# Transposed attention weights and two modulation parts of layer 0, in a two-layer DiT block on one Trainium2 core

## The chip, the cores and the metric

The kernel runs on one NeuronCore of a Trainium2 chip. The metric is device time in microseconds (us) of one execution, lower is better. The kernel before takes 2725.24 us, the median of three runs (2724.99 to 2725.42).

## The reference, cut to what matters

Everything is float32. Two layers work on `x` (1024 tokens by 1024 channels); the first also reads a context of 256 tokens. Each layer takes six modulation vectors (shift, scale, gate for the mixer; the same for the experts) from a conditioning vector:

```python
def adaln(cond, w, b):                       # w: 1024 x 6144 per layer
    m = jax.nn.silu(cond) @ w + b
    return jnp.split(m[..., None, :], 6, axis=-1)

sh1, sc1, gt1, sh2, sc2, gt2 = adaln(c, w_mod[layer], b_mod[layer])
hx = modulate(x, norm_mix_g[layer], sh1, sc1)     # rmsnorm(x)*(1+scale)+shift
...                                               # layer 0: mLSTM heads and window attention
p = jax.nn.softmax(jnp.concatenate([s_loc, s_ctx, s_sink], axis=-1), axis=-1)
out = einsum(p[..., :w3], vw) + einsum(p[..., w3:], vc)
...
x = x + gt1 * yx
x = x + gt2 * ec_moe(modulate(x, norm_ffn_g[layer], sh2, sc2), *moe)
```

Window attention has 8 heads of width 64, blocks of 128 queries, and for each block up to 3 x 128 local keys, 256 context keys and a sink that enters the sum of the softmax only. Layer 1's mixer is a chunked gMLP. Both layers end in a mixture of 16 experts.

## The kernel before, in words

To keep float32 accuracy at one pass per column, a large operand is split into a high part (type fp32r, written by ScalarE) and the rest (low part, by VectorE or GpSimd), and a product is three matmuls: high x high, low x high, high x low. Small products stay plain float32.

The program is written in a framework that traces it and then orders each engine's instructions itself: a planner with estimated costs takes, on each engine, the first ready instruction in the order of the text, and sets the semaphores. Each engine and each DMA queue (SP, ACT, POOL) then runs its list in order. So the text gives priorities, not the final order. A tile pool has a number of buffers per tag; a new tile waits until a buffer of that tag is released by its last reader.

**Start** (`start`, L182). Two context tiles and eight tiles of rows of `x`, each 128 x 1024, lie in the pool `xp`, tag `xt`, ten buffers (L185, L190). `start_mod` (L259) computes shift and scale of the first mixer: eight weight tiles of 1 MB on SP's queue, 32-column float32 matmuls (L272), and at k = 2 the transposes of the context (L166). Then `heads_context` (L219) projects the context for four heads: per head a key and a value projection (`proj`, L298, 24 matmuls of 256 columns each), a convolution on VectorE, and a store. Each projection's weight is 512 KB on SP's queue into a ring of two (`wraw`), split by ScalarE (L70) and VectorE (L71). Between projections, two of sixteen row steps are issued (`more`, L245, L254): four transposes (L213) of 128 columns of the rows, and the modulated copy, split (L174 to L179). A half of the rows (four `xt` tiles) is read until its eighth step.

**Attention** (`layer0_a` L551, `attention` L445). For each of 4 pairs of heads and 8 query blocks: scores of two heads into two-bank PSUM tiles (L462 to L466), row maximum (L472), exponential with sum (L475), reciprocal of the sum (L478). Then `dg`, the identity scaled by that column (L480), and a plain float32 product of each 128 x 128 tile of exponentials `P` with `dg` (L492), which transposes and scales at once, back into the score tile. The result is split (L494, L495) and multiplied by the values (L501, L502). There are 4 or 5 such tiles for a head and block, 304 in all.

Between these steps `fill` issues other work: 288 projection steps of three matmuls (query, head inputs, gates) in portions of 4, 2 and 3 a block, and with 9 of 28 of them one step of the modulation. `mod_part` (L660) computes one of the ten remaining vectors (layer 0 parts 2 to 5, layer 1 parts 0 to 5): eight steps, each a 512 KB weight tile `wm` on POOL's queue (ring of two, L667) and four 32-column float32 matmuls (L670), and a ninth step that adds the bias (L676) and either stores the vector (parts 2 and 5) or transposes it into columns (L683, L684).

```python
            mods = itertools.chain(*(self.mod_part(lm, pa, pt, i // 6, i % 6) for i in range(2, 12)))
            def fill(n):
                for _ in itertools.islice(work, n):
                    i = next(steps)
                    if 9 * (i + 1) // 28 > 9 * i // 28:
                        next(mods, None)
```

After attention come the mLSTM (`layer0_b`), the experts of layer 0, the gMLP and the experts of layer 1.

Of the kernel before, what the change touches and what calls it, by code (L numbers as in the profile page):

```python
# [8 lines left out]
F32 = mybir.dt.float32  # L9
# [4 lines left out]
ALU = mybir.AluOpType  # L14
# [7 lines left out]
KD = 8  # L22
# [16 lines left out]
class Kernel:  # L39
# [142 lines left out]
    def start(self, rings):  # L182
        nc, I = self.nc, self.I
        with ExitStack() as late:
# [29 lines left out]
                        self.modulated(ps, k, sm, gs[:, 0, :], mc[:, 0, 0:8], self.hH[:, k, sl], self.hL[:, k, sl])  # L214
                        yield

            self.heads_context(late, pt, Ws, rows())

    def heads_context(self, s, pt, Ws, more):  # L219

        nc = self.nc
        hc = (self.cH, self.cL)
# [12 lines left out]
        for hd in range(4):  # L235
            W = Ws.pop(0) if Ws else self.w_in(512 + hd * 128)
            acc = self.pa.tile([128, 512], F32, tag="acc", name="acc")
            self.proj(acc[:, :NCTX], W, hc, 0, NCTX)
            pad = cpool.tile([128, NCTX + 4], F32, tag="cpad", name="cpad")
            nc.vector.memset(pad[:, 0:2], 0.0)  # L240
            nc.vector.memset(pad[:, NCTX + 2:NCTX + 4], 0.0)
            nc.scalar.activation(pad[:, 2:2 + NCTX], acc[:, :NCTX], AF.Copy)
            kc = cpool.tile([128, NCTX], F32, tag="kcT", name="kcT")
            self.conv_silu(pad, NCTX, 4 + hd, kc)
            list(itertools.islice(more, 2))  # L245
            W = Ws.pop(0) if Ws else self.w_in(1024 + hd * 128)
            acc = self.pa.tile([128, 512], F32, tag="acc", name="acc")
            self.proj(acc[:, :NCTX], W, hc, 0, NCTX)
            vc = cpool.tile([128, NCTX], F32, tag="vcT", name="vcT")
            nc.scalar.activation(vc, acc[:, :NCTX], AF.Copy)  # L250
            if kept:
                store(*kept)
            kept = hd, kc, vc
            list(itertools.islice(more, 2))  # L254
        store(*kept)
        for _ in more:
            pass

    def start_mod(self, cs, cT, sm, pt):  # L259
# [185 lines left out]
    def attention(self, hp, c, Q, fill):  # L445
# [6 lines left out]
        for n in range(NT):  # L452
# [17 lines left out]
            for i in range(2):  # L470
# [16 lines left out]
            for i in range(2):  # L487
                if i:
                    fill(self.FILLS[1])
                P, dg = Ps[i]  # L490
                for j in range(nt):
                    nc.tensor.matmul(S[i][:, 512 - nl + j * 128:640 - nl + j * 128], P[:, j * 128:(j + 1) * 128], dg, start=True, stop=True)  # L492
# [58 lines left out]
    def layer0_a(self, rings):  # L551
        nc, I = self.nc, self.I
        with ExitStack() as s:
# [60 lines left out]
            mods = itertools.chain(*(self.mod_part(lm, pa, pt, i // 6, i % 6) for i in range(2, 12)))  # L614
# [4 lines left out]
            def fill(n):  # L619

                for _ in itertools.islice(work, n):
                    i = next(steps)
                    if 9 * (i + 1) // 28 > 9 * i // 28:
                        next(mods, None)

            for c in range(4):
# [30 lines left out]
                                        kh[base:base + 64, c0:c0 + n].bitcast(F32), op=ALU.subtract)  # L657


    def mod_part(self, pool, pa, pt, layer, w):  # L660


        nc, I = self.nc, self.I
        acc = pa.tile([128, 512], F32, tag="acc", name="acc")[:, 0:256]
        for k in range(KD):
            wm = pool.tile([128, D], F32, tag="wm", name="wm")
            nc.gpsimd.dma_start(out=wm, in_=I["w_mod"][layer, k * 128:(k + 1) * 128, D * w:D * (w + 1)])  # L667
            lhs = self.silw[:, k].rearrange("p a s -> p (a s)")
            for j in range(4):
                nc.tensor.matmul(acc[32 * j:32 * j + 32, :], lhs, wm[:, 256 * j:256 * (j + 1)], start=(k == 0), stop=(k == KD - 1))  # L670
            yield
        rows = pool.tile([128, 256], F32, tag="mrows", name="mrows", bufs=1)
        bias = pool.tile([128, 256], F32, tag="mbias", name="mbias", bufs=1)
        b = I["b_mod"]
        nc.gpsimd.dma_start(out=bias, in_=bass.AP(tensor=b.tensor, offset=b.offset + 6 * D * layer + D * w, ap=[[256, 4], [0, 32], [1, 256]]))
        nc.vector.tensor_tensor(rows, acc, bias, op=ALU.add)  # L676
        if w % 3 == 2:
            i = 2 * layer + w // 3
            nc.gpsimd.dma_start(out=self.s_gt[i].rearrange("(j c) -> j c", j=4), in_=rows[0:128:32, :])
        else:  # L680
            tr = pt.tile([128, 512], F32, tag="tr", name="tr")
            for t in range(2):
                nc.tensor.transpose(tr[:, t * 128:(t + 1) * 128], rows[:, t * 128:(t + 1) * 128], self.ident)  # L683
            nc.vector.tensor_copy(self.modc[:, layer, 8 * w:8 * w + 8].rearrange("p (j t) -> p j t", t=2),  # L684
                                  tr[:, 0:256].rearrange("p (t j r) -> p j t r", t=2, j=4)[:, :, :, 0])
        yield


# [1012 lines left out]
```

## Time and profile before

| | |
|---|---|
| median of 3 runs | 2725.24 us (2724.99 to 2725.42) |
| the profiled execution | 2720.4 us, span 2718.6 us, mean granted clock 0.968 |
| TensorE (PE) busy | 2529.9 us, 93% of the span |
| VectorE (DVE) / ScalarE (ACT) / GpSimd (POOL) busy | 1879.9 / 1511.4 / 626.0 us |
| chain that ended last, by engine | PE 80%, DVE 8%, DMA 4%, issue 4%, ACT 3% |
| start, to about 104 us; attention, about 165 to 590 us | inside the span |

PE is busy nearly everywhere, and records of matmuls overlap: what a matmul costs is the distance between starts, not its own duration. PEld is the load of weights, which overlaps. PEclk is TensorE's granted clock as a share of 2.4 GHz (0.5 is 1.2 GHz). "x8" is a merged group of records; a 128-column plain float32 product leaves two records, a transpose one.

### The profile page before, as it was taken

What the parts mean: (1) busy time and instruction counts of PE and PEld (TensorE: products, weight loads), DVE (VectorE), ACT (ScalarE), POOL (GpSimd) and SP (SyncE); (2) the same over time, 40 slices, a digit from 0 to 9 for tenths busy, and PEclk for the clock granted to TensorE, in tenths of its full rate; (3) what the DMA queues carried; (4) which work ended last, traced back from release to release, by engine and by line L of the source; (5) the groups of instructions that cost most, each with busy time, mean ns of one, the idle gap of its engine ahead of it and who ended that gap; (6) DMA issues with size and microseconds to landing.
All of it is one profiled execution on the core that took longest, in us unless ns stands there. A gap on an engine that the chain in (4) does not pass through costs nothing.

```text
span 2718.6 us, 35149 instructions
## 1 busy us (share of the span) xinstructions
PE 2529.9 (93%) x12847; PEld 2005.4 (74%) x12847; DVE 1879.9 (69%) x2830; ACT 1511.4 (56%) x2258; POOL 626.0 (23%) x413
## 2 busy tenths in 40 slices
PE   5999999998895999999998999999995999999996
PEld 3767777777774788888776887888884788888774
DVE  5566656567737999999885184116505899999887
ACT  4344344334424888888775223232322888888774
POOL 0010111115421222221102434533451021231001
PEclk8999999999996999999999999999997999999998
DMA  7344554457166999999966323342335999999995
GB/s 261 103 128 141 152 160 142 144 185 265 48 238 234 352 388 380 387 380 386 374 215 202 101 67 119 117 147 70 101 108 190 376 373 388 380 381 382 359 363 186
DMA packets 241642, 644.02 MB, mean 237 GB/s; under 512 B 18609, under 2 KB 85341, under 8 KB 240445
## 3 DMA queue, kind: packets, MB, share of 16 engines
q1 hardware_dynamic: 205136, 530.52, 52.3%
q0 software_dynamic: 25840, 89.99, 11.7%
q10 hardware_dynamic: 10492, 21.26, 2.3%
q8 instruction: 101, 1.65, 0.2%
q14 instruction: 73, 0.59, 0.1%
HBM read 589.06 MB, written 50.02 MB: 235 GB/s over the span
## 4 chain that ended last, share of the span: by engine, by line
PE 80%; DVE 8%; DMA 4%; issue 4%; ACT 3%; POOL 1%; POOLq 0%; ACTq 0%; SPq 0%; DVEq 0%
PE g L1134 13%; PE u L1134 13%; PE d L1134 12%; PE acc L298 8%; PE acc L1444 7%; PE acc L1518 6%; PE acc L1466 6%; PE S L492 2%; PE acc L805 2%; PE acc L670 2%; DMA wm<-in_w_mod_dram 1%; PE tr L1164 1%; DVE s2k L1460 1%; PE tr L1208 1%; PE O L501 1%
## 5 line engine op out<-in xcount | busy, mean ns | idle before, releaser
L71 DVE TENSOR_TENSOR ml<-mraw,mh 128x1024 fp32r<-128x1024 f32 x750 | 875.3, 1222 | 61.7 <-ACT mh L70 61.2
L70 ACT ACTIVATE mh<-mraw 128x1024 fp32r<-128x1024 f32 x750 | 769.3, 1064 | 138.6 <-PE g L1134 67.8
L71 POOL TENSOR_TENSOR wl<-wraw,wh 128x1024 fp32r<-128x1024 f32 (+1 forms) x132 | 253.6, 1930 | 349.8 <-ACT wh L70 349.8
L70 ACT ACTIVATE wh<-wraw 128x1024 fp32r<-128x1024 f32 (+1 forms) x163 | 143.0, 893 | 311.0 <-issue 123.6
L1232 POOL DMA_INDIRECT s_x<-xe,idx x28 | 66.9, 2388 | 655.0 <-ACT hidH L1210 394.4
L1134 PE MATMUL g<-mh,xH 128*128 128x512 f32 x512 | 206.4, 403 | 1.4 <-ACT xH L1169 1.4
L1134 PE MATMUL g<-ml,xH 128*128 128x512 f32 x512 | 205.3, 401 | 1.5 <-DVE ml L71 1.4
L1134 PE MATMUL g<-mh,xL 128*128 128x512 f32 x512 | 204.4, 399 | 0.0
L1134 PE MATMUL u<-ml,xH 128*128 128x512 f32 x512 | 203.4, 397 | 0.2
L1134 PE MATMUL u<-mh,xL 128*128 128x512 f32 x512 | 202.2, 395 | 0.0
L1134 PE MATMUL u<-mh,xH 128*128 128x512 f32 x512 | 202.2, 395 | 0.0
L1134 PE MATMUL d<-ml,hidH 128*128 128x512 f32 x496 | 197.5, 398 | 5.0 <-DVE ml L71 4.9
L1152 POOL DMA_INDIRECT xe<-s_xr,idx x32 | 137.7, 4303 | 270.7 <-ACT mh L70 131.0
L1134 PE MATMUL d<-mh,hidH 128*128 128x512 f32 x496 | 198.2, 400 | 1.6 <-DVE o L1229 1.6
L1134 PE MATMUL d<-mh,hidL 128*128 128x512 f32 x496 | 196.3, 396 | 0.0
L1444 PE MATMUL acc<-wh,h2k 128*128 128x512 f32 x512 | 163.7, 400 | 1.8 <-DVE h2k L1426 1.7
L1466 PE MATMUL acc<-h2k,wh 128*128 128x512 f32 x512 | 161.5, 396 | 0.0
L298 PE MATMUL acc<-hH,wh 128*128 128x512 f32 (+1 forms) x368 | 155.4, 422 | 1.6 <-DVE mrows L676 0.5
L1518 PE MATMUL acc<-wh,s2k 128*128 128x512 f32 x480 | 152.1, 397 | 0.0
L298 PE MATMUL acc<-hL,wh 128*128 128x512 f32 (+1 forms) x368 | 145.7, 396 | 0.0
L298 PE MATMUL acc<-hH,wl 128*128 128x512 f32 (+1 forms) x368 | 145.7, 396 | 0.0
L667 POOL DMA_DIRECT2D wm<-in_w_mod_dram x80 | 42.7, 534 | 406.6 <-PE acc L670 382.1
(469 smaller groups left out, 5238.9 us busy)
## 6 DMA issues: line engine op xcount, KB each, us to landing
mraw<-in_moe_w_down_dram SPq DMA_DIRECT2D x128, 1024.0 KB
mraw<-in_moe_w_gate_dram SPq DMA_DIRECT2D x126, 1024.0 KB
mraw<-in_moe_w_up_dram SPq DMA_DIRECT2D x124, 1024.0 KB
wm<-in_w_mod_dram POOLq DMA_DIRECT2D x80, 512.0 KB, 4.2
wraw<-in_gm_w_in_dram SPq DMA_DIRECT2D x64, 512.0 KB
wraw<-in_gm_w_out_dram SPq DMA_DIRECT2D x32, 512.0 KB
wraw<-in_ab_w_in_dram SPq DMA_DIRECT2D x30, 512.0 KB
wm<-in_w_mod_dram SPq DMA_DIRECT2D x8, 1024.0 KB
```

What stands on the lines that cost most here:

```text
L70: nc.scalar.activation(h, src, AF.Copy)
L71: i = (nc.gpsimd if eng == "pool" else nc.vector).tensor_tensor(l, src, h.bitcast(F32), op=ALU.subtract)
L298: nc.tensor.matmul(acc, a[:, k, :], b[:, k, c0:c0 + n], start=(k == 0 and i == 0), stop=(k == KD - 1 and i == 2))
L492: nc.tensor.matmul(S[i][:, 512 - nl + j * 128:640 - nl + j * 128], P[:, j * 128:(j + 1) * 128], dg, start=True, stop=True)
L670: nc.tensor.matmul(acc[32 * j:32 * j + 32, :], lhs, wm[:, 256 * j:256 * (j + 1)], start=(k == 0), stop=(k == KD - 1))
L805: nc.tensor.matmul(acc, a[:, k, t * 128:(t + 1) * 128], b[:, k % 2, :], start=(k == 0 and i == 0), stop=(k == 3 and i == 2))
L1134: nc.tensor.matmul(acc[:, sl], a[:, k, :], b[:, sl], start=(k == 0 and i == 0), stop=(k == KD - 1 and i == 2))
L1152: f = nc.gpsimd.indirect_dma_start(out=xe, out_offset=None, in_=self.s_xr[layer], in_offset=bass.IndirectOffsetOnAxis(ap=self.idx[e], axis=0))
L1232: nc.gpsimd.indirect_dma_start(out=self.s_x[layer], out_offset=bass.IndirectOffsetOnAxis(ap=self.idx[e], axis=0), in_=o, in_offset=None, c ...
L1444: nc.tensor.matmul(acc[t], a[k][:, ts], b[:, k2, :], start=(k == 0 and i == 0), stop=(k == KD - 1 and i == 2))
L1466: nc.tensor.matmul(acc, a[:, k, :], b[k], start=(k == 0 and i == 0), stop=(k == KD - 1 and i == 2))
L1518: nc.tensor.matmul(acc, a[:, ts], b[k2], start=(c == 0 and i == 0), stop=(c == 15 and i == 2))
```

## The change

Three edits. The tiles `P` are scaled by VectorE, in place, and then transposed plainly. Parts 2 and 3 of layer 0 (gate of the mixer, shift of the experts) leave attention's `fill` and are issued between the context projections, their weight tiles in the buffers of `xt`, their sums in a PSUM pool of their own. In attention one modulation step goes with every fourth projection step, for the eight parts that are left. `mod_part` is also cut into helpers (`mod_step`, `mod_bias`, `mod_columns`) with the same instructions, and the bias is now fetched just after the eighth step.

```diff
@@ start
-            self.heads_context(late, pt, Ws, rows())
+            pm = self.pool(late, "pmod0", space=PSUM)
+            mods = itertools.chain(*(self.mod_part(xp, "xt", sm, pm, pt, 0, w) for w in (2, 3)))
+            self.heads_context(late, pt, Ws, rows(), mods)
@@ heads_context, after the key's convolution / after the value's projection / at the end
             list(itertools.islice(more, 2))
+            list(itertools.islice(mods, (1, 1, 3, 3)[hd]))
...
             list(itertools.islice(more, 2))
+            list(itertools.islice(mods, (0, 2, 3, 3)[hd]))
         store(*kept)
-        for _ in more:
+        for _ in itertools.chain(more, mods):
             pass
@@ attention
-                dg = hp.tile([128, 128], F32, tag="dg", name="dg", bufs=2)
-                nc.vector.tensor_scalar(dg, self.ident, den, None, op0=ALU.mult)
-                Ps.append((P, dg))
+                Ps.append((P, den))
             fill(self.FILLS[0])
...
-                P, dg = Ps[i]
+                P, den = Ps[i]
+                nc.vector.tensor_scalar(P[:, 0:w], P[:, 0:w], den, None, op0=ALU.mult)
                 for j in range(nt):
-                    nc.tensor.matmul(S[i][:, ...], P[:, j * 128:(j + 1) * 128], dg, start=True, stop=True)
+                    nc.tensor.transpose(S[i][:, ...], P[:, j * 128:(j + 1) * 128], self.ident)
@@ layer0_a
-            mods = ... self.mod_part(lm, pa, pt, i // 6, i % 6) for i in range(2, 12)
+            mods = ... self.mod_part(lm, "wm", lm, pa, pt, i // 6, i % 6) for i in range(4, 12)
...
-                    i = next(steps)
-                    if 9 * (i + 1) // 28 > 9 * i // 28:
+                    if next(steps) % 4 == 3:
                         next(mods, None)
@@ mod_part
         for k in range(KD):
-            wm = pool.tile([128, D], F32, tag="wm", name="wm")
+            wm = wp.tile([128, D], F32, tag=tag, name="wm")
             nc.gpsimd.dma_start(out=wm, in_=...)
...
```

## Rows read from the trace of the kernel before

**Rows 1.** The busy times of stretches of the span: length, then busy time and record count of PE, PEld, DVE, ACT and POOL, then granted clock, DMA share and GB/s.
```profile
22.00:36.00 14.00, 7.47 (x52) 1.29 (x50) 1.49 (x5) 0.46 (x1) 0.00 (x0) 0.88 1.03 340
...
50.00:63.00 13.00, 11.58 (x89) 10.19 (x90) 12.97 (x23) 11.98 (x23) 0.00 (x0) 1.00 0.31 84
63.00:68.00 5.00, 1.60 (x9) 1.19 (x8) 5.00 (x9) 3.59 (x7) 0.00 (x0) 0.89 0.14 53
68.00:82.00 14.00, 13.71 (x106) 13.24 (x106) 12.17 (x35) 5.15 (x8) 0.00 (x0) 0.92 0.55 150
82.00:94.00 12.00, 5.63 (x35) 4.58 (x34) 11.06 (x19) 8.68 (x16) 0.34 (x2) 0.72 0.35 94
...
165.00:590.00 425.00, 419.69 (x2728) 317.87 (x2726) 258.34 (x556) 169.44 (x355) 50.06 (x90) 1.00 0.48 149
```
**Rows 2.** The waits of PE from 165 to 590 us: waiting line, what it waited for, us in total, times, longest.
```profile
PE S L492 <- DVE ast L477: 1.7, 1, 1.7
PE acc L670 <- DMA wm<-in_w_mod_dram: 0.9, 3, 0.4
PE S L492 <- DVE dg L480: 0.6, 2, 0.4
```
**Rows 3.** All products of P with dg, and all modulation steps with their weight transfers (durations min/median/max in ns, first and last start; the last line in us).
```profile
L492 PE MATMUL S<-dg,P x608: 270/275/422, 175.4 to 580.8; 128*128 128x128 f32 x152
...
L670 PE MATMUL acc<-wm,silw x640: 379/379/404, 150.4 to 570.8; 128*32 128x256 f32 x160
L667 POOL DMA_DIRECT2D wm<-in_w_mod_dram x80: 527/528/696, 104.6 to 563.3; - x80
...
DMA to landing us min/median/max: 3.8/4.2/7.5
```
**Rows 4.** The timeline of one block of attention: start in us, duration, engine, line, what.
```profile
291.03 0.39 PE L298 MATMUL acc<-hL,wh 128*128 128x512 f32 x1
...
291.26 0.40 PE L298 MATMUL acc<-hH,wl 128*128 128x512 f32 x1
...
291.59 0.64 PE L670 MATMUL acc<-wm,silw 128*32 128x256 f32 x8
...
292.15 0.50 PE L298 MATMUL acc<-hH,wh 128*128 128x512 f32 x1
...
292.50 0.40 PE L298 MATMUL acc<-hL,wh 128*128 128x512 f32 x1
...
293.46 0.29 DVE L480 TENSOR_SCALAR dg<-cst,ast 128x128 f32<-128x128 f32 x1
...
294.45 0.64 PE L670 MATMUL acc<-wm,silw 128*32 128x256 f32 x8
...
295.02 1.38 PE L492 MATMUL S<-dg,P 128*128 128x128 f32 x10
...
296.16 0.47 PE L298 MATMUL acc<-hH,wh 128*128 128x512 f32 x1
```
**Rows 5.** The timeline of PE at transposes of a head's context: the first of four that follow each other, and what comes right behind the fourth.
```profile
58.99 0.27 PE L228 MATMUL tr<-cst,kcT 128*128 128x128 f32 x1
...
59.42 0.60 PE L213 MATMUL tr<-cst,xt 128*128 128x128 f32 x4
```
**Rows 6.** Groups of VectorE instructions: line, operation, count | busy us, mean ns of one | idle before. The first of 165 to 590 us, the other two of 36 to 104 us.
```profile
L480 DVE TENSOR_SCALAR dg<-cst,ast 128x128 f32<-128x128 f32 x64 | 18.1, 286 | 3.8 <-issue 2.3
...
L157 DVE TENSOR_SCALAR xt<-xt,rsq_y 128x1024 f32<-128x1024 f32 x8 | 5.7, 750 | 0.0
L312 DVE TENSOR_SCALAR kcT<-cpad,convw 128x256 f32<-128x256 f32 x4 | 1.4, 352 | 1.7 <-ACT cpad L242 1.7
```
**Rows 7.** The timeline of another block, where dg is ready and the product starts.
```profile
281.13 0.29 DVE L480 TENSOR_SCALAR dg<-cst,ast 128x128 f32<-128x128 f32 x1
...
281.56 0.46 PE L492 MATMUL S<-dg,P 128*128 128x128 f32 x2
```
**Rows 8.** The timeline of the first modulation's last two weights of 1 MB on PE, and the last transposes of the context before.
```profile
20.21 2.28 PE L166 MATMUL tr<-cst,xt 128*128 128x128 f32 x15 [0.25 <-DVE xt L157]
...
31.30 1.07 PE L272 MATMUL mod<-wm,silw 128*32 128x512 f32 x8 [1.75 <-DMA wm<-in_w_mod_dram]
33.82 1.94 PE L272 MATMUL mod<-wm,silw 128*32 128x512 f32 x8 [1.45 <-DMA wm<-in_w_mod_dram]
```
**Rows 9.** The waits of PE from 36 to 104 us, in us in total, times, longest.
```profile
PE tr L213 <- ACT hmod L174: 2.9, 2, 2.5
PE acc L298 <- DVE wl L71: 2.6, 3, 2.1
```
**Rows 10.** The timeline of PE at the eighth row step, the last of the first half of the rows, and at the sixteenth.
```profile
62.55 0.60 PE L213 MATMUL tr<-cst,xt 128*128 128x128 f32 x4
...
89.28 1.12 PE L213 MATMUL tr<-cst,xt 128*128 128x128 f32 x4 [2.45 <-ACT hmod L174]
```
**Rows 11.** A projection's weight: its issue on SP's queue and its split on ScalarE.
```profile
77.53 0.37 SPq L78 DMA_DIRECT2D wraw<-in_ab_w_in_dram  x1
...
81.39 1.06 ACT L70 ACTIVATE wh<-wraw 128x1024 fp32r<-128x1024 f32 x1 [1.96 <-DMA wraw<-in_ab_w_in_dram]
```
**Rows 12.** A stretch in which 18 of PE's 20 records are transposes of the rows (L213), columns as in the first group.
```profile
50.70:54.80 4.10, 2.96 (x20) 2.06 (x20) 4.07 (x9) 4.07 (x8) 0.00 (x0) 1.00 0.01 2
```

More of the change, by code (lines that the diff above doesn't have):

```diff
@@ L215, in rows, with heads_context @@
                         yield
-            self.heads_context(late, pt, Ws, rows())
-    def heads_context(self, s, pt, Ws, more):
+            pm = self.pool(late, "pmod0", space=PSUM)
+            mods = itertools.chain(*(self.mod_part(xp, "xt", sm, pm, pt, 0, w) for w in (2, 3)))
+            self.heads_context(late, pt, Ws, rows(), mods)
+    def heads_context(self, s, pt, Ws, more, mods):
         nc = self.nc
@@ L489, in attention @@
                     fill(self.FILLS[1])
-                P, dg = Ps[i]
+                P, den = Ps[i]
+                nc.vector.tensor_scalar(P[:, 0:w], P[:, 0:w], den, None, op0=ALU.mult)
                 for j in range(nt):
-                    nc.tensor.matmul(S[i][:, 512 - nl + j * 128:640 - nl + j * 128], P[:, j * 128:(j + 1) * 128], dg, start=True, stop=True)
+                    nc.tensor.transpose(S[i][:, 512 - nl + j * 128:640 - nl + j * 128], P[:, j * 128:(j + 1) * 128], self.ident)
                 src = S[i][:, row].rearrange("p (j q) -> p j q", q=128)
@@ L613, in layer0_a @@
             Qs = [Q, [], [], []]
-            mods = itertools.chain(*(self.mod_part(lm, pa, pt, i // 6, i % 6) for i in range(2, 12)))
+            mods = itertools.chain(*(self.mod_part(lm, "wm", lm, pa, pt, i // 6, i % 6) for i in range(4, 12)))
             work = itertools.chain(*(itertools.chain(self.query(pa, qp, c + 1, hx, Qs[c + 1]) if c < 3 else (),
@@ L657, in key_stack, with mod_step, mod_bias @@
                                         kh[base:base + 64, c0:c0 + n].bitcast(F32), op=ALU.subtract)
-    def mod_part(self, pool, pa, pt, layer, w):
-        nc, I = self.nc, self.I
+    def mod_step(self, acc, k, wm):
+        for j in range(4):
+            self.nc.tensor.matmul(acc[32 * j:32 * j + 32, :], self.silw[:, k].rearrange("p a s -> p (a s)"), wm[:, 256 * j:256 * (j + 1)],
+                                  start=(k == 0), stop=(k == KD - 1))
+    def mod_bias(self, pool, layer, w, bufs=1):
+        b = self.I["b_mod"]
+        bias = pool.tile([128, 256], F32, tag="mbias", name="mbias", bufs=bufs)
+        self.nc.gpsimd.dma_start(out=bias, in_=bass.AP(tensor=b.tensor, offset=b.offset + 6 * D * layer + D * w, ap=[[256, 4], [0, 32], [1, 256]]))
+        return bias
@@ new lines, in mod_columns, with mod_part @@
+    def mod_columns(self, rows, pt, layer, w, copy):
+        tr = pt.tile([128, 512], F32, tag="tr", name="tr")
+        for t in range(2):
+            self.nc.tensor.transpose(tr[:, t * 128:(t + 1) * 128], rows[:, t * 128:(t + 1) * 128], self.ident)
+        copy(self.modc[:, layer, 8 * w:8 * w + 8].rearrange("p (j t) -> p j t", t=2),
+             tr[:, 0:256].rearrange("p (t j r) -> p j t r", t=2, j=4)[:, :, :, 0])
+    def mod_part(self, wp, tag, pool, pa, pt, layer, w):
+        nc = self.nc
@@ L664, in mod_part @@
         acc = pa.tile([128, 512], F32, tag="acc", name="acc")[:, 0:256]
         for k in range(KD):
-            wm = pool.tile([128, D], F32, tag="wm", name="wm")
[L667 to L670, printed above, removed]
+            wm = wp.tile([128, D], F32, tag=tag, name="wm")
@@ L671, in mod_part @@
+            nc.gpsimd.dma_start(out=wm, in_=self.I["w_mod"][layer, k * 128:(k + 1) * 128, D * w:D * (w + 1)])
+            self.mod_step(acc, k, wm)
             yield
+        bias = self.mod_bias(pool, layer, w)
         rows = pool.tile([128, 256], F32, tag="mrows", name="mrows", bufs=1)
-        bias = pool.tile([128, 256], F32, tag="mbias", name="mbias", bufs=1)
-        b = I["b_mod"]
-        nc.gpsimd.dma_start(out=bias, in_=bass.AP(tensor=b.tensor, offset=b.offset + 6 * D * layer + D * w, ap=[[256, 4], [0, 32], [1, 256]]))
@@ L680, in mod_part @@
         else:
[L681 to L685, printed above, removed]
+            self.mod_columns(rows, pt, layer, w, nc.vector.tensor_copy)
         yield
```

## The prediction

> **What bounds the kernel now.** I read the stretches of busy time first, for where PE has room. From 165 to 590 us, attention with its filled-in projections, PE is busy 419.7 of 425 us at a granted clock of 1.00, VectorE 258 and ScalarE 169 [rows 1]; and the list of PE's waits has 3.2 us in all there [rows 2]. So attention lasts as long as PE's list, and a microsecond of PE work taken out is a microsecond, until something else ends last. The start is another case: from 50 to 94 us PE is idle 1.4, 3.4, 0.3 and 6.4 us, 11.5 in all, at clocks down to 0.72, while VectorE is busy 12.97 of 13, 5 of 5, 12.2 of 14 and 11.1 of 12 [rows 1], and PE's longest waits are on the modulated copies and the split weights [rows 9]. There VectorE and ScalarE set the pace. Before that, from 22 to 36 us, the DMA engines are full (share 1.03, 340 GB/s) [rows 1] and PE waits for the first modulation's weights [rows 8]. Then I read the timeline, for prices from start to start, since PE's records overlap.
>
> **The transposes.** All 608 records of the products with dg are 304 tiles, two records each [rows 3]. A group of five tiles takes 296.16 - 295.02 = 1.14 us from its start to the next line's [rows 4], 0.228 a tile; without a hand-over of some 0.1 us, 0.208. Four transposes of the same size take 59.42 - 58.99 = 0.43 us, 0.107 each [rows 5]. The hand-over stays, so a tile saves 0.10 to 0.12 us. I take one record, 0.107: 304 x 0.107 = **32.5 us** off PE's list (30 to 36).
>
> **The scaling.** dg's 128 columns cost 286 ns. The price of P's 512 or 640 is not in the trace; between 256 columns (352 ns) and 1024 (750 ns) [rows 6] a column is 0.518 ns, so 0.485 and 0.551 us. With 16 tiles of the one and 48 of the other the mean is 0.535, 0.25 more than dg: 64 x 0.25 = 16 us on VectorE. Beside the 258 of [rows 1] that is 274 in some 385 us, so VectorE doesn't become the bound by its sum.
>
> **Two parts out of attention.** A modulation step lies between two projection matmuls that start at 291.26 and 292.50; the distance without it is 0.23 (291.03 to 291.26), so the step costs 1.24 - 0.46 = 0.78 us with both hand-overs [rows 4]. Two parts are 16 such steps, 12.5 us, and the two transposes of part 3 are 0.2: **12.7 us** off. The steps that are left come at one in four instead of 9 in 28, so their weights have more time to land (4.2 us [rows 3]); PE's 0.9 us of waits on them is small change [rows 2]. The helpers and the earlier fetch of the bias cost nothing: POOL is busy 50 of 425 us [rows 1], and the bias is behind eight weights.
>
> **What comes back in attention.** Fewer steps and a longer VectorE instruction eat the time between the scores and the transposes. Four projection steps carry 4 x (9/28 - 1/4) = 0.29 steps fewer, 0.22 us; the scaling adds 0.25. In the block of [rows 4] dg is ready at 293.75 and PE comes at 295.02: 1.27 us of room, with two modulation steps in it. In that of [rows 7] it is ready at 281.42 and PE starts at 281.56, no room at all. If half of the 32 blocks are like the second and lose 0.4 us, that is **6 us**. Bounds: 0, where the planner finds other matmuls for the gap, and 32 x (0.47 + 0.25) = 23, where no block has room, for either head.
>
> **What the start pays.** Three terms. First, the two context buffers are free after the transposes at 22.5 us, so POOL issues the first two weights (2 x 0.53 us on its queue [rows 3]) into full DMA engines. The last two weights of 1 MB come 33.82 - 31.30 = 2.52 us apart [rows 8]; 1 MB more ahead of the last delays everything behind it by 2.5 us. Bounds 0 (they are served last) to 2.5; I take 2.5, since two buffers' worth on another queue does not wait for SP's. The Trainium skill (DMA: Bandwidth & Descriptors, section Queues, rings and completion order) says that each DMA engine goes round the queues that have work, packet by packet; by that the price is the 2.5 us, and were it not so, 0. Second, the 16 steps on PE: 12.5 us at 0.78, into 11.5 us of idle [rows 1]. Where the planner puts them and when their weights land decides. Weights three to six need the first half of the rows, free after the eighth row step at 62.55 us; the other buffers of rows come free at 89.28 [rows 10], but steps already done free theirs sooner. So some 9 us of 12.5 can lie in idle time, and 3.5 are paid. Third, 7 MB more transfers beside the projections' weights, which are on the path at least once: issued at 77.53, split at 81.39 after a wait of 1.96 us [rows 11]. Four such loads, each slowed by up to its own 512 KB at 340 GB/s, 1.5 us, are 6 at most; I take 1. SP's queue itself gets nothing. On VectorE come two sums and one copy of under 0.5 us each, hidden or 1 us at most. Sum **7 us**. Bounds: 12.5 + 6 + 2.5 = 21, nothing hidden; and a gain of 3, since PE at 0.72 of its clock for 12 us [rows 1] has 3.4 us to win if the new steps keep it busy.
>
> **The sum.** -32.5 - 12.7 + 6 + 7 = -32.2 us against the profiled execution's 2720.4: 2688. The median of the runs is 4.8 us higher, so **2693 us**. What comes after attention has no clock of its own: its transfers are released by buffers, so it moves along.
>
> **The rivals.** (a) *Attention becomes a chain.* The wait for the scaled P ends last in every block, 23 instead of 6: 2710. For it: no room in [rows 7]; against: 3.2 us of waits in 425 [rows 2], and a planner that fills. 0.09. (b) *The start hides nothing*: 21 instead of 7, 2707. For it: full DMA engines before 36 us and a busy VectorE; against: PE's idle time and DMA shares of 0.14 to 0.55 after 50 us [rows 1]. 0.13. (c) *The transposes of P are no cheaper than the products*, so the change doesn't do what it says: 2693 + 32.5 = 2725.5, no change. Against: every transpose shown leaves one record 0.107 us apart [rows 5]. 0.03. (d) *Slower: POOL's queue runs the new weights one at a time.* If the planner gives each of the last 14 weights the buffer that the step just before releases, each step waits for issue and landing, 0.53 + 4.2 us at best and 0.53 + 7.5 at worst [rows 3], and PE's list stands behind it. From 62.55 us on, 14 x 8 = 112 us reach to 175 instead of 104, 71 later: 2693 - 7 + 74 = 2760. It turns to a loss where (14 x step) passes 41 + 39 us, from 5.7 us a step. Against: ten buffers, of which four come free together. 0.03. (e) *The clock falls in attention.* [rows 12] has a clock of 1.00 in a stretch nearly all of transposes, right behind matmuls, so I see no sign of it. The Trainium skill (TensorE: Matmul & The Clock Gate, section Part 4: PE-mode transpose) says that the full clock does not engage for transposes; the trace does not agree there. If each group of transposes ran at 1.2 GHz with the rest of its block's projections behind it (five steps of 0.69 us), 64 x 0.5 + 32 x 3.5 = 144 us come on top: 2837. 0.02.
>
> **How the numbers follow.** The forecast has 0.70, by its own bounds 2680 to 2704. The range is 2680 to 2711: it takes in (a) and (b), and leaves out (c), (d), (e) and the corners of the bounds. A measurement of this kernel can tell about 0.2%, 5.4 us, from no change. Faster by more: 0.70 + 0.09 + 0.13 = 0.92. Same: (c), 0.03. Slower: (d) and (e), 0.05.
>
> **What would show it.** Right: the line of the transposes in attention has 304 records instead of 608; the last attention record comes some 33 us earlier than 590; PE's waits in attention stay under 10 us; the modulation's records before 104 us number a fifth of all. The scaling's mean is near 0.54 us. Each term can be read alone: the end of the first modulation (33.82 before) gives the 2.5, the last context projection the rest of the 7. Wrong: waits of PE on new weights in the start of over 10 us; a granted clock under 1.00 in attention; waits of the transposes on the scaling of over 20 us.

## The result, and the profile after

The changed kernel takes 2700.74 us (median of three, 2699.18 to 2702.14) against 2725.24: 24.5 us faster, ratio 0.991, interval 0.9887 to 0.9932. Forecast were 2693 and a range of 2680 to 2711. The profiled execution has a span of 2697.4 us against 2718.6.

The same stretches as in [rows 1], by what happens in them (columns as there):
```profile
22.00:38.00 16.00, 9.11 (x58) 2.04 (x56) 2.33 (x8) 0.25 (x1) 1.10 (x2) 0.79 1.03 368
...
52.00:65.00 13.00, 12.46 (x95) 9.63 (x96) 12.31 (x28) 9.78 (x19) 1.14 (x2) 1.00 0.58 168
65.00:70.00 5.00, 3.05 (x31) 2.09 (x29) 4.17 (x10) 4.12 (x8) 3.13 (x6) 1.00 0.35 78
70.00:84.00 14.00, 12.02 (x82) 9.62 (x82) 9.93 (x24) 3.81 (x6) 1.67 (x3) 0.76 1.07 375
84.00:96.00 12.00, 12.00 (x107) 8.96 (x107) 8.85 (x14) 5.20 (x10) 2.93 (x5) 1.00 0.80 238
96.00:108.00 12.00, 6.12 (x50) 3.26 (x49) 9.05 (x18) 6.73 (x11) 0.35 (x2) 0.79 0.39 110
...
175.00:572.00 397.00, 383.55 (x2350) 287.95 (x2349) 275.31 (x574) 172.80 (x365) 40.97 (x72) 1.00 0.46 142
```
Attention is still PE's, at a granted clock of 1.00. The DMA engines are full from 70 to 84 us now, and PE's idle time near 96 to 108 us has stayed, although it has 16 modulation steps more to do. The transposes, the modulation steps and the scaling, which answer to [rows 3] and [rows 6]:
```profile
L495 PE MATMUL S<-cst,P x304: 270/273/332, 188.6 to 557.6; 128*128 128x128 f32 x152
...
L665 PE MATMUL acc<-wm,silw x640: 379/379/637, 54.0 to 551.4; 128*32 128x256 f32 x160
...
L493 DVE TENSOR_SCALAR P<-P,ast 128x640 f32<-128x640 f32 (+1 forms) x64 | 34.0, 537 | 1.5
```
304 records instead of 608, the scaling at 537 ns where 535 was interpolated, and modulation steps from 54 us on. PE's waits from 165 to 575 us, which answer to [rows 2]:
```profile
PE acc L665 <- DMA wm<-in_w_mod_dram: 8.5, 7, 2.4
PE S L495 <- DVE ast L481: 1.7, 2, 1.0
PE S L495 <- DVE P L493: 1.3, 2, 0.6
```
The wait for the modulation's weights was 0.9 us and is 8.5. Five marks in PE's timeline split the difference (us):

| mark | before | after | difference |
|---|---|---|---|
| first modulation's last weight | 33.82 | 35.96 | +2.1 |
| first context projection | 40.19 | 42.33 | +2.1 |
| last row step | 89.28 | 99.38 | +10.1 |
| first 512-column projection | 103.79 | 118.76 | +15.0 |
| last projection beside attention | 595.53 | 571.30 | -24.2 |

So the start lost 15.0 us, and "attention" (below always from the first 512-column projection to the last) went from 491.7 to 452.5 us, 39.2 less. Behind it both kernels take the same within 3 us (2123.1 and 2126.1); in the traces of the experiments this rest, which lies behind all edits, is 2121.6 to 2135.1 us. The first mark has a spread too: without moved parts it lies at 32.2 to 33.8 us in four traces, with them at 35.7 to 37.4 in ten.

Two places hold the start's loss. One is a burst of weights. These lines are PE's and POOL's, from two timelines of the changed kernel:
```profile
66.83 3.13 POOL L688 DMA_DIRECT2D wm<-in_w_mod_dram  x6 [8.99 <-PE acc L665]
...
67.77 0.28 PE L302 MATMUL acc<-cL,wh 128*128 128x256 f32 x1
71.16 0.64 PE L665 MATMUL acc<-wm,silw 128*32 128x256 f32 x8 [3.12 <-DMA wm<-in_w_mod_dram]
72.62 1.06 PE L665 MATMUL acc<-wm,silw 128*32 128x256 f32 x2 [0.82 <-DMA wm<-in_w_mod_dram]
```
As soon as buffers come free, six weights are asked for at once, and PE's list has a step that needs one of them only 1 us later. PE's next matmuls then ran at the lower of its two clocks, 1.2 GHz:
```profile
73.61:78.61 5.00, 5.00 (x24) 4.78 (x23) 1.53 (x9) 0.00 (x0) 0.00 (x0) 0.50 1.04 409
```
The projections' own weights become late beside these transfers. The next lines are SP's, ScalarE's and VectorE's:
```profile
88.26 0.37 SPq L78 DMA_DIRECT2D wraw<-in_ab_w_in_dram  x1
...
97.61 1.06 ACT L70 ACTIVATE wh<-wraw 128x1024 fp32r<-128x1024 f32 x1 [5.53 <-DMA wraw<-in_ab_w_in_dram]
98.57 0.76 ACT L174 ACTIVATE hmod<-tr,mc,gs 128x512 f32<-128x512 f32 x1
...
98.70 1.23 DVE L71 TENSOR_TENSOR wl<-wraw,wh 128x1024 fp32r<-128x1024 f32 x1 [4.87 <-ACT wh L70]
```
Paired in the order of the queue, the weight asked for at 88.26 us is the one that is split at 97.61: 9.35 us, against 3.9 in [rows 11]. The four weights issued from 71.9 to 91.3 us took 9.0 to 9.6 us each. ScalarE and VectorE both stand still for this one, and the modulated copy (L174) that the last row step waits for comes right behind the split. The other place is the tail behind the last row:
```profile
99.38 1.08 PE L213 MATMUL tr<-cst,xt 128*128 128x128 f32 x4 [2.66 <-ACT hmod L174]
100.39 3.13 PE L665 MATMUL acc<-wm,silw 128*32 128x256 f32 x32
...
105.48 0.41 PE L677 MATMUL tr<-cst,mrows 128*128 128x128 f32 x2 [1.21 <-DVE mrows L693]
107.81 0.58 PE L302 MATMUL acc<-cH,wh 128*128 128x256 f32 x1 [1.91 <-DVE modc L678]
```
The last four steps of part 3, its bias sum, its transposes and its copy stand between the last row and the next projection. That copy is queued on VectorE behind a split and two differences (L71 at 105.25, L179 at 106.39; the copy at 107.59). From the last row step to the next projection it is 8.4 us, against 4.0 before.

From the first context projection to the first 512-column one, PE is busy 64.9 of 76.4 us, where it was busy 50.9 of 63.6. Its work there grew by 14.0 us and its idle time fell by only 1.1, from 12.7 to 11.5 us.

### The profile page after: what moved, and what is told of

It reads as the page before. It is cut to its first block, busy times and chain, and to the rows that moved or that the text cites. A ratio compares the mean times of both kernels' runs of the same rounds, so it can differ in the third digit from the quotient of the medians.

```text
span 2697.4 us, 34523 instructions
## 1 busy us (share of the span) xinstructions
PE 2499.7 (93%) x12543; PEld 1974.5 (73%) x12543; DVE 1893.6 (70%) x2830; ACT 1511.4 (56%) x2258; POOL 629.6 (23%) x413
## 4 chain that ended last, share of the span: by engine, by line
PE 76%; DVE 7%; issue 7%; DMA 5%; ACT 2%; POOL 1%; POOLq 0%; SPq 0%; ACTq 0%; DVEq 0%
PE g L1147 13%; PE u L1147 13%; PE d L1147 12%; PE acc L1457 7%; PE acc L302 7%; PE acc L1531 6%; PE acc L1479 6%; PE acc L818 2%; DMA wm<-in_w_mod_dram 2%; PE acc L665 1%; PE S L495 1%; PE tr L1177 1%; PE tr L1221 1%; DVE s2k L1473 1%; PE acc L1491 1%
## 5 line engine op out<-in xcount | busy, mean ns | idle before, releaser
L71 DVE TENSOR_TENSOR ml<-mraw,mh 128x1024 fp32r<-128x1024 f32 x750 | 875.3, 1222 | 62.0 <-ACT mh L70 61.4
L71 POOL TENSOR_TENSOR wl<-wraw,wh 128x1024 fp32r<-128x1024 f32 (+1 forms) x132 | 257.9, 1963 | 345.6 <-ACT wh L70 342.0
L1245 POOL DMA_INDIRECT s_x<-xe,idx x28 | 55.4, 1979 | 664.8 <-ACT hidH L1223 414.0
L1165 POOL DMA_INDIRECT xe<-s_xr,idx x32 | 146.3, 4571 | 265.1 <-ACT mh L70 123.4
```

What stands on the lines that cost most here:

```text
L71: i = (nc.gpsimd if eng == "pool" else nc.vector).tensor_tensor(l, src, h.bitcast(F32), op=ALU.subtract)
L1165: f = nc.gpsimd.indirect_dma_start(out=xe, out_offset=None, in_=self.s_xr[layer], in_offset=bass.IndirectOffsetOnAxis(ap=self.idx[e], axis=0))
L1245: nc.gpsimd.indirect_dma_start(out=self.s_x[layer], out_offset=bass.IndirectOffsetOnAxis(ap=self.idx[e], axis=0), in_=o, in_offset=None, c ...
```

## The experiments

Each difference is against the median of the kernel before, measured together with it (2722.3 to 2725.2); "attention" and the start's end (first 512-column projection) are from the profiled execution. Two rows that were measured apart can differ by some us for that reason alone: e5, with the changed kernel's attention time and a start within 2 us of its own, gained 19.6 us where that one gained 24.5.

| run | time | against before | ratio, interval | start's end | attention |
|---|---|---|---|---|---|
| before | | | | 103.8 | 491.7 |
| changed kernel | 2700.7 | -24.5 | 0.991 (0.9887 to 0.9932) | 118.8 | 452.5 |
| e1 transposes only | 2707.0 | -17.0 | 0.9938 (0.9925 to 0.9951) | 103.3 | 476.1 |
| e2 moved parts only | 2726.9 | +2.9 | 1.0011 (1.0002 to 1.0020) | 119.6 | 474.4 |
| e3 unscaled | 2692.6 | -31.4 | 0.9878 (0.9862 to 0.9893) | 119.3 | 440.3 |
| e4 half tiles | 2704.8 | -19.2 | 0.9923 (0.9910 to 0.9936) | 121.1 | 458.1 |
| e5 scaling early | 2703.4 | -19.6 | 0.9922 (0.9901 to 0.9943) | 120.7 | 452.4 |
| e6 resident weights | 2682.3 | -40.7 | 0.9845 (0.9823 to 0.9868) | 118.3 | 434.6 |
| e7 own ring | 2708.2 | -14.9 | 0.9938 (0.9914 to 0.9961) | 128.8 | 454.5 |
| e8 gate last | 2693.1 | -29.9 | 0.9887 (0.9867 to 0.9908) | 112.8 | 452.3 |
| e9 transposes, resident | 2682.3 | -40.8 | 0.9862 (0.9847 to 0.9877) | 101.6 | 452.9 |
| e10 pairs | 2693.2 | -29.9 | 0.9895 (0.9879 to 0.9910) | 112.9 | 450.3 |
| e11 three parts | 2710.4 | -12.7 | 0.9961 (0.9947 to 0.9974) | 127.8 | 452.5 |
| e12 before, resident | 2713.4 | -8.9 | 0.9968 (0.9956 to 0.9979) | 102.6 | 483.0 |

**e1, the transposes alone.**
```diff
-                dg = ...; nc.vector.tensor_scalar(dg, self.ident, den, ...)
+                # on the kernel before: scale P in place behind the fill, transpose(S, P, ident)
```


> The kernel before with the scaling of P and the plain transposes alone; all ten modulation parts stay in attention at nine of 28. Theory A (the terms add, and the start's 15 us come from the moved steps alone): the start ends where it ended before (first 512-column projection near 103.8 us) and attention is shorter by 32.5 us less 0 to 4 us of waits, so 28 to 33 us faster than the kernel before, 2692 to 2697, and faster than the changed kernel by 4 to 9 us. Rival B (the transposes alone run into the wait for the scaled P, and the changed kernel only gained because of the moved steps): under 24 us, slower than 2701.

17.0 us faster, attention 15.6 shorter: Rival B's number, and half of what the records' count promises. The waits of its PE from 100 to 600 us:
```profile
PE acc L669 <- DMA wm<-in_w_mod_dram: 10.4, 13, 2.0
PE num L748 <- DVE nP L743: 5.1, 2, 3.6
PE S L491 <- DVE ast L477: 2.1, 1, 2.1
...
PE S L491 <- DVE P L489: 0.6, 2, 0.3
```
The scaled P is waited for 0.6 us, the modulation's weights 10.4 (the second line lies behind attention). So it has B's time, but not B's place.

**e2, the moved parts alone.** The product with `dg` put back into the changed kernel.
```diff
+                dg = hp.tile([128, 128], F32, ...); nc.vector.tensor_scalar(dg, self.ident, den, ...)
-                nc.vector.tensor_scalar(P[:, 0:w], P[:, 0:w], den, None, op0=ALU.mult)
-                    nc.tensor.transpose(S[i][...], P[...], self.ident)
+                    nc.tensor.matmul(S[i][...], P[...], dg, start=True, stop=True)
```

> The changed kernel with the product with dg put back; the two parts stay in the start and the cadence is one in four. Theory A: the start pays the same 15 us (first 512-column projection near 118.8 us), attention gives back 12.7 us less some 5 us of waits on the weights' ring, so 2 to 8 us slower than the kernel before, 2727 to 2733. Rival C (moving the parts is worth its 12.7 us and the start's loss comes from something else): 2715 to 2722.

2.9 us slower, as Theory A had it. The start pays 15.8 us, attention is 17.3 shorter. Moving the parts is nothing by itself. But e1 and e2 add up to 14 us and the changed kernel gained 24.5; in attention they add up to 32.9 us, and it gained 39.2. Each makes the other worth more.

**e3, the scaling left out.**
```diff
-                nc.vector.tensor_scalar(P[:, 0:w], P[:, 0:w], den, None, op0=ALU.mult)
```


> The changed kernel without the scaling of P: the exponentials are transposed as they are, so the softmax is not divided by its sum. It prices the scaling (0.54 us on VectorE, 64 times) where it stands. Theory A (VectorE has room and the planner fills the gap): at most the 3 us that the transposes wait for VectorE in the trace of the changed kernel, 0 to 4 us faster than it. Rival B (a chain behind the scaled P): the 16 to 34 us that the scalings take come off in good part, over 8 us faster.

8.1 us less than the changed kernel by the medians, 6.9 by the differences in the table, 12.2 in attention: more than the 3.0 us that its transposes wait for VectorE, on the edge of what Rival B asked for, and less than its whole chain. PE's waits for the modulation's weights fall with it, from 8.5 to 5.3 us, so not all of it is the scaling's own time.

**e5, the scaling ahead of the fill.**
```diff
                 nc.vector.reciprocal(den, den)
+                nc.vector.tensor_scalar(P[:, 0:w], P[:, 0:w], den, None, op0=ALU.mult)
                 Ps.append((P, den))
             fill(self.FILLS[0])
...
-                nc.vector.tensor_scalar(P[:, 0:w], ...)
```


> The changed kernel with the scaling of P moved ahead of the fill, right behind the reciprocal, where dg was built before: the same 64 instructions, but with priority over the convolutions, splits and rotations that the fill puts on VectorE. Theory B2 (the 8 us that leaving the scaling out was worth are its wait behind that work, not its own time): 4 to 8 us faster than the changed kernel, 2693 to 2697. Theory B3 (they are its own 0.54 us, 0.25 more than dg's, in every block's chain): 0 to 3 us faster.

Attention 452.4 against 452.5: nothing. The traces say why. In both kernels the scaling starts 0.04 us, the median of 64, behind the reciprocal that it needs, so the planner had it there already and the edit moved next to nothing. The scaling does not stand behind the fill's work, and Theory B2 falls. That it costs by its own length in the chain (B3) is what is left; this run does not show it.

**e4, half tiles.**
```diff
-        lm = self.pool(rings, "lm", bufs=2, side="right")
+        lm = self.pool(rings, "lm", bufs=5, side="right")     # tiles of 128 x 512, two transfers a step
```


> The changed kernel with attention's modulation weights in halves: five tiles of 256 KB instead of two of 512 KB, so that two steps and a half are fetched ahead and each half is free after two of its four matmuls. It takes away the 8.5 us that PE waits for these weights in attention. Theory A (the ring of two is what those waits are): waits under 2 us and 5 to 9 us faster than the changed kernel. Rival D (the weights are late because POOL's queue or the DMA engines are slow, not because the buffer is free too late): no faster, or slower, since POOL issues twice as many transfers.

No faster, and the waits on the weights are still 7.4 us (from 100 to 600 us):
```profile
PE acc L697 <- DMA wm<-in_w_mod_dram: 7.4, 6, 2.3
...
PE S L495 <- DVE P L493: 3.8, 3, 1.7
```
A ring half a step deeper with twice the transfers (landing 3.6 us in the median instead of 4.2) does not help. It changes depth and number of transfers together, so it does not separate the two, and a deeper ring of whole tiles was not run. What a wait is made of can be read in the trace of the changed kernel, on PE and on POOL:
```profile
429.76 0.64 PE L665 MATMUL acc<-wm,silw 128*32 128x256 f32 x8
430.73 0.53 POOL L688 DMA_DIRECT2D wm<-in_w_mod_dram  x1 [5.73 <-PE acc L665]
433.28 0.64 PE L665 MATMUL acc<-wm,silw 128*32 128x256 f32 x8
435.72 0.64 PE L665 MATMUL acc<-wm,silw 128*32 128x256 f32 x8 [1.80 <-DMA wm<-in_w_mod_dram]
```
The third step needs the buffer of the first. POOL had been waiting for that buffer and asked for the next weight as soon as it was free; 5.0 us later the step could start. Of the seven waits six are like this one: issued 0.7 us behind the start of the last matmul on the buffer, and wanted before issue and landing were over. So POOL's queue is not late by itself, as Rival D had it: the buffer comes free too late for a step that follows so soon.

**e6, resident weights.** From the third step of attention on, no weight is fetched:
```diff
+            if tag == "xt" or len(self.kept) < 2:
                 wm = wp.tile(...); nc.gpsimd.dma_start(out=wm, ...)
+            else:
+                wm = self.kept[k % 2]
```


> The changed kernel with attention's modulation steps on two weight tiles that are fetched once and stay: the eight vectors of attention are computed from the wrong weights. It takes away 62 transfers of 512 KB, their issues on POOL and the wait for them, and leaves every matmul. Theory W (PE's waits for these weights, 8.5 us by the changed kernel's trace, are what attention lost against the sum): waits on weights gone in attention, 6 to 10 us faster than the changed kernel. Rival (the waits only take the place of others, on VectorE and ScalarE): under 4 us faster.

Attention falls by 17.9 us to 434.6, the time by 18.4 by the medians, twice the waits that are named in the trace and more than Theory W's 6 to 10. From 165 to 575 us PE waits no more for weights:
```profile
PE num L769 <- DVE nP L764: 5.1, 2, 3.6
PE S L495 <- DVE ast L481: 2.0, 1, 2.0
PE num L769 <- ACT nb L771: 1.2, 1, 1.2
```
(The lines on `num` lie behind attention.) Fetching weights while attention runs holds it more than the scaled P does: with all scalings in place, attention is shorter here than in e3. The busy times of attention, of the changed kernel and of this one (columns as in [rows 1]), tell where the 17.9 us were:
```profile
118.76:571.30 452.54, 437.90 (x2609) 326.49 (x2607) 302.40 (x613) 191.17 (x388) 44.10 (x77) 1.00 0.45 137
118.31:552.86 434.55, 429.48 (x2609) 328.18 (x2608) 301.99 (x613) 191.57 (x388) 10.04 (x15) 1.00 0.22 68
```
PE's idle time falls from 14.6 to 5.1 us, and its busy time by 8.4 us with as many records. The order of the steps explains the second part. Counted in the two traces, the 64 modulation steps lie in 64 groups between other matmuls in the changed kernel and in 41 here, where a step need not wait for its weight. A group costs about 0.62 us at its two edges (from the start of the matmul before it to its first, and from its last to the next), the hand-overs of the prediction, and two projection matmuls without it 0.23 [rows 4], so 23 groups fewer are worth some 9 us by this estimate.

**e9 and e12, resident weights with and without the transposes, all ten parts in attention.** The edit of e6 on e1, and on the kernel before.

> The kernel with the transposes alone, with attention's modulation steps on two weight tiles that are fetched once: all ten vectors are computed from the wrong weights. It asks where the transposes' other 17 us went, of 32.5 on PE's list, when all ten parts stay in attention. Theory W (with 80 weights to fetch in a shorter attention, the ring of two sets the pace): attention from the first 512-column projection to the last falls from 476 us to 440 to 455, and the time to 2670 to 2685. Rival B (VectorE's chain to the scaled P sets it): 465 or more, and 2697 or more.

> The kernel before, products with dg and all, with attention's modulation steps on two weight tiles that are fetched once: all ten vectors are computed from the wrong weights. Against the transposes alone with the same resident weights (attention 452.9 us, 2682.3 us) it prices the transposes where no weight is waited for. Theory W (the transposes are worth their 32.5 us, and with fetched weights the ring takes half of it): attention 481 to 489 us, 4 to 10 us faster than the kernel before, so 28 to 36 us over the run with transposes. Rival (the transposes are worth 17 us whatever the weights, and resident weights are worth 23 us in any kernel): attention near 470 us, 20 or more us faster than the kernel before.

Both by Theory W. Here are the four cells, attention in us:

| ten parts in attention | product with dg | transposes | transposes are worth |
|---|---|---|---|
| weights fetched | 491.7 | 476.1 | 15.6 |
| weights resident | 483.0 | 452.9 | 30.1 |
| fetching costs | 8.7 | 23.2 | |

With no weight to wait for, the transposes are worth 30.1 us of the 32.5 on the list (31.1 by the medians). With 80 weights to fetch, half of it is lost. These are the busy times of attention in the four cells: before and e1, then e12 and e9:
```profile
103.79:595.53 491.74, 485.54 (x3043) 364.50 (x3041) 289.49 (x616) 192.25 (x388) 53.70 (x96) 1.00 0.47 144
103.29:579.35 476.06, 459.62 (x2738) 329.02 (x2737) 303.83 (x616) 191.60 (x388) 54.64 (x96) 0.99 0.49 148
102.61:585.62 483.01, 482.89 (x3042) 365.35 (x3041) 289.63 (x616) 192.01 (x388) 11.94 (x18) 1.00 0.20 62
101.57:554.45 452.88, 448.40 (x2738) 329.82 (x2737) 302.69 (x616) 191.45 (x388) 12.55 (x18) 1.00 0.21 66
```
With fetches the transposes take 25.9 us off PE's busy time and add 10.2 us of idle time; without, they take 34.5 off and add 4.4. So the loss is partly a new wait and partly the order: the steps lie in 87 groups before and 94 in e1, in 81 in e12 and 75 in e9. The kernel before paid 8.7 us for its fetches, though only 0.9 of it is listed as a wait of PE for weights in [rows 2]; its idle time in attention was 6.2 us and is 0.1 in e12.

**e7, a ring of two of its own in the start.**
```diff
-            mods = ... self.mod_part(xp, "xt", sm, pm, pt, 0, w) for w in (2, 3)
+            wq = self.pool(late, "wq", bufs=2)
+            mods = ... self.mod_part(wq, "wq", sm, pm, pt, 0, w) for w in (2, 3)
```


> The changed kernel with the start's modulation weights in a ring of two buffers of their own instead of the buffers of the rows. No more than 1 MB is under way at a time, so the burst of seven weights near 67 to 73 us goes. Theory S (the burst makes the projections' weights late and PE waits for it): the start ends 3 to 6 us earlier than the changed kernel's 118.8 us. Rival (the start is long because of the steps' own PE time and the tail behind the last row): within 2 us of it, or later, since a ring of two feeds PE one weight at a time.

The start ends 10 us later (128.8). The burst is gone, but PE waits 15.0 us for the modulation's weights from 45 to 119 us, where the changed kernel waits 4.3 from 36 to 119:
```profile
PE acc L666 <- DMA wm<-in_w_mod_dram: 15.0, 8, 4.8
PE acc L303 <- DVE wl L71: 2.2, 1, 2.2
```
Half of Theory S holds: without the burst the projections' weights take 4.0 to 4.9 us from issue to split again, instead of 9.0 to 9.6. But a ring of two costs more by its own waits than it gives back, so the rows' buffers are the better place, burst and all.

**e8, the gate part last.**
```diff
-            mods = ... for w in (2, 3)
+            mods = ... for w in (3, 2)
```


> The changed kernel with the two parts of the start in the other order: the shift of the experts first, the gate of the mixer last. The part that ends the start is then stored and not transposed, so the chain sum on VectorE, two transposes, copy on VectorE is not behind the last row. Theory T (the next projection waits for that copy, 1.2 + 1.9 us in the trace): the first 512-column projection starts 2 to 4 us earlier than at 118.8 us. Rival (something else, the last split weight, ends last there): no change.

The start ends at 112.8, 5.9 us earlier than in the changed kernel; in the other kernels with the changed kernel's start (e2 to e6) it ends at 118.3 to 121.1. PE's timeline at the last row:
```profile
100.33 1.04 PE L213 MATMUL tr<-cst,xt 128*128 128x128 f32 x8
101.30 1.91 PE L665 MATMUL acc<-wm,silw 128*32 128x256 f32 x26
...
103.73 0.63 PE L665 MATMUL acc<-wm,silw 128*32 128x256 f32 x6
104.29 0.39 PE L302 MATMUL acc<-cH,wh 128*128 128x256 f32 x1
```
The last row step is the second half of the first line, at 100.77 us, so it is 3.5 us from there to the projection, against 8.4. The projections that follow ran at another clock. These are PE's first us of them, in the changed kernel and here:
```profile
107.81:112.00 4.19, 4.19 (x19) 4.19 (x20) 0.74 (x5) 0.00 (x0) 0.00 (x0) 0.50 0.88 243
104.29:108.00 3.71, 3.71 (x34) 3.71 (x32) 3.18 (x10) 0.55 (x2) 0.59 (x1) 1.00 0.64 189
```
Here they start 0.117 us apart, at the full 2.4 GHz. In the changed kernel, and in the kernel before, PE had been idle ahead of them and they began 0.213 us apart, at 1.2 GHz. From the first projection to the end of the start it is 8.5 us instead of 11.0. So the two waits are not the whole gain: 4.9 us less behind the last row and 2.4 less by the clock, against a last row that comes 1.4 later. By the medians this kernel is 10.3 us faster than e5, measured together with it, and, with e10, the fastest of those that leave out none of the work.

**e10, pairs, and e11, three parts**, both on e8.
```diff
# e10
-                    if next(steps) % 4 == 3:
-                        next(mods, None)
+                    if next(steps) % 8 == 7:
+                        list(itertools.islice(mods, 2))
# e11
-            mods = ... for w in (3, 2)
+            mods = ... for w in (3, 4, 2)          # and 7 of 32 in attention
```


> The kernel with the gate part last, with two modulation steps after every eighth projection step in attention instead of one after every fourth: as many steps and weights, in pairs. Theory W: a pair finds both weights landed, since 8 projection steps of 0.69 us and what lies between are longer than two issues and a landing (5.3 us), and one of two hand-overs of 0.2 us goes, so 4 to 12 us faster than the kernel with the gate part last, 2681 to 2689. Rival (the planner orders the steps by its own estimates, whatever the text asks for): within 3 us of it.

Within 0.1 us of e8. The waits on weights from 165 to 575 us fall from 8.9 to 4.9 us, and those on the scaled P rise from 1.4 to 4.9:
```profile
PE S L495 <- DVE P L493: 4.9, 7, 1.8
PE acc L665 <- DMA wm<-in_w_mod_dram: 4.9, 3, 1.8
```
The text was followed: the steps lie in 48 groups instead of 64, and PE's busy time in attention falls by 3.2 us. But its idle time grows by 1.1, since one wait takes the place of the other. So Rival's number came, and not its reason.

> The kernel with the gate part last, with a third part (the scale of the experts of layer 0) in the start as well, and seven parts in attention, seven steps in 32. From the runs so far two parts out of attention were worth 23.6 us there, 11.8 each, and cost 9 us in the start, 4.5 each. Theory W: 3 to 8 us faster than the kernel with the gate part last, 2685 to 2690. Rival (PE's idle time in the start is used up, so that a third part costs its full 6 us of PE and more of DMA there): no faster, 2692 to 2700.

Slower: the start ends at 127.8, 15 us later than with two parts, and attention is not shorter at all (452.5, with 10.4 us of waits on weights). A third part costs the start more than it gives back in attention.

## Why the prediction was right

Time, sign and range held, and the likeliest case came, but in part by luck. Of the span 21.2 us were won where 32.2 were forecast. Of the 11.0 missing, 8.0 are the start's term, and 3.0 lie behind attention, where the change does nothing. Attention gave 39.2 us, and 32.5 + 12.7 - 6 is 39.2 as well. That it fits to the tenth is luck: none of these three terms has its own size, and the errors cancel.

- **What bounds it**: right. Attention is PE's list, the start is not. With resident weights the list's saving arrives nearly whole (30.1 of 32.5). The 3.2 us of waits are those of the three longest lines; PE's idle time there was 5.3 us by [rows 1].
- **The transposes**: the price per tile was right, 0.107 us. The claim that a microsecond out of PE's list is a microsecond was not: alone they gave 15.6 us, between e2 and the changed kernel 21.9, without fetches 30.1. The step that failed is "the steps that are left ... have more time to land ... small change". In e1 all ten parts stay, and the weights become the wait; in the changed kernel it is 8.5 us instead of 0.9. "Until something else ends last" was said, and what that would be was there to be read in [rows 3], issue 0.53 and landing 4.2 us. It was held against the mean cadence of the steps only. The step that waits at 435.72 us was reached 4.2 us after the start of the step that had used its buffer last, and issue and landing take longer than that.
- **Two parts out of attention**: 12.7 by the list; 17.3 measured with the product (491.7 to 474.4) and 23.6 with the transposes (476.1 to 452.5). Nearly all of it is PE's busy time, 21.7 of the 23.6 us, and not a wait for fetches. What was mis-sized is, at least in part, the number of hand-overs: 16 steps left, but by the new order the steps lie in 25 groups fewer with the product (87 to 62) and 30 fewer with the transposes (94 to 64). At 0.39 us a group the 9 and 14 beyond the 16 are 3.5 and 5.5 us, of the 4.6 and 10.9 that came on top; the rest is not traced. So what the first term lost, this one gave back.
- **What comes back in attention**: 6 us were put down as a chain to the scaled P. The place was wrong. The trace lists 3.0 us on the scaled P and its sum, against 2.3 before, and 8.5 on weights. The scaling as a whole is worth 7 to 12 us (e3), but not by its place in the text (e5).
- **What the start pays**: 7 forecast, 15.0 measured, inside the bound of 21. The delay of the first modulation was 2.1 us for 2.5 in the two profiled executions, so POOL's transfers were not served last; over all traces the two groups of kernels lie 1.9 to 5.2 us apart. The Trainium skill (DMA: Bandwidth & Descriptors, section Queues, rings and completion order) says that each DMA engine goes round the queues that have work. The trace agrees. The step that failed is "some 9 us of 12.5 can lie in idle time": PE's work there grew by 14.0 us and its idle time fell by 1.1, so next to nothing was hidden. New waits took the place of the old ones, 4.3 us on the new weights among them. The price of late weights was wrong as well. Each load was to be slowed by 1.5 us at most, and four were slowed by some 5 us (9.0 to 9.6 us instead of 3.7 to 4.5), with ScalarE and VectorE waiting. At the end, part 3's chain through VectorE adds 4.4 us behind the last row. e8 takes 5.9 us away by the order of two parts alone, with which the start pays 9.0.
- **The signs**: 304 records, 0.54 us for a scaling, and a fifth of the modulation's records before 104 us came as told. PE's listed waits in attention were to stay under 10 us and are 11.5; the last records of attention were to come 33 us earlier and came 24.2 earlier.
- **The rivals**: (b), an unhidden start, is what came in the start: its 12.5 and 2.5 us are the 15.0 measured, without the 6 for the projections' weights. (a) did not come as told. (c), (d) and (e) did not come: 304 records, six weights asked for at once, and a granted clock of 1.00 from 175 to 572 us. The Trainium skill (TensorE: Matmul & The Clock Gate, section Part 4: PE-mode transpose) says that the full clock does not engage for transposes. With 304 of them amid matmuls the trace does not agree.

What stays open: whether a ring of three or more whole tiles would end the waits for weights in attention. No run has one, and half tiles and pairs did not end them. The planner's order differs in each of these kernels; the count of groups shows that it matters, but no run changes the order alone.

## What to carry to other kernels

Work taken out of a PE-bound stage counts in full only until the next stream that feeds the stage is late. So after the sum, go through the streams with a fixed turn-round (here issue, landing and a ring of two) and test them against the closest uses of one buffer, not the mean distance. The order counts as well: where a planner can put small steps next to each other, the hand-overs between them go. And "idle time" is not free room. Look at what the new work's result waits for, since a part that ends in a chain through another engine costs more at the end of a stage than one that ends in a store, and at whose transfers its own data will delay.

## What the runs showed of the hardware

- A 128 x 128 float32 transpose on PE leaves one record and takes 0.107 us from start to start; the product with a diagonal leaves two and takes about twice that (0.208 to 0.228 us). Over 304 tiles that made 30.1 us where nothing else was late.
- Two modulation weights of 512 KB on POOL's queue, issued while SP's queue kept the DMA engines full, delayed SP's last transfer by 2.1 us in the pair of traces compared.
- A weight of 512 KB on SP's queue took 3.7 to 4.5 us from issue to split from 56 us on in the kernel before, 9.0 to 9.6 us beside POOL's transfers in the changed kernel, and 4.0 to 4.9 us where POOL had a ring of two (e7).
- After PE had been idle, projections of 256 columns began 0.213 us apart at a granted clock of 0.50, and 0.117 us apart later in the same stretch, or at once when PE had not been idle (e8, clock 1.00). The tail's cost comes once as a wait and once more as clock.
